# Sliding-window extraction: VectorE's plain row copies go from identity shuffles to copies, and one of them takes ScalarE's quarter

## The chip, the cores and the metric

The kernel runs on one core of a Trainium2 chip. The metric is the device time of one execution in microseconds; three runs of the kernel before took 187.24, 187.06 and 187.02 us, a median of 187.06 us.

Three engines matter here: VectorE (DVE), ScalarE (ACT) and GpSimd (POOL). TensorE does nothing. POOL issues most of the DMAs, SyncE (SP) and ACT the rest. Sixteen DMA engines move the bytes between device memory and the on-chip memory (SBUF), which has 128 partitions.

## The reference

The input `x` has 16 images of 64 channels of 64 x 64 float32. Every 8 x 8 window with stride 4 is copied out, 15 x 15 windows per image, each with all channels:

```
n_h = (h - window_size) // stride + 1
n_w = (w - window_size) // stride + 1
result = np.zeros((batch, n_h, n_w, c, window_size, window_size), dtype=np.float32)
for i in range(n_h):
    for j in range(n_w):
        h_start = i * stride
        w_start = j * stride
        result[:, i, j] = x[:, :, h_start:h_start + 8, w_start:w_start + 8].copy()
```

Nothing is calculated; it is a movement of data. The input is 16.78 MB and the output 58.98 MB, as neighbouring windows overlap: 3600 windows (16 x 225) of 64 x 8 x 8 float32, 16384 bytes each. One window is one row of the output when that is seen as a matrix, and is contiguous there.

## The kernel before

**The input on chip.** The tile `L` holds all of `x`. Each image is cut into 4 bands of 16 image rows (`HQ = 4`) and 2 halves of 32 channels (`CH = 2`). Partition `ch*64 + b*4 + q` holds channel half `ch` of image `b`, band `q`: 32 channels x 16 rows x 64 columns. The loads are issued by POOL, SP and ACT at the start (`load`, L58, and L112); the first channels of each partition come by way of two of the output buffers and are copied into `L` at L126.

**The output buffers.** There are four, `G0` to `G3`, used in turn by `tile_()`. A buffer has 128 partitions of one whole window each (64 channels x 8 x 8, 16384 bytes). So one buffer takes 128 windows, and one store, an indirect DMA issued by POOL (L138, `scatter`), writes each partition to the output row that an index list gives (`idx_y`, `idx`, `idx_lo`, `idx_hi`). A row whose index lies beyond the output is dropped. A buffer is filled again only when its store has landed, which the framework enforces with semaphores.

**The tiles in their order.** With `s` the number of a window's first row within the band in units of 4 (0 to 3) and `j` the window's column:

- *Parts* (`part`, L197), six of them: the windows of half of the images for two columns and `s` = 0 and 1. Each is 8 copies of 32 partitions, 3 by ACT and 5 by DVE. The first three are made as soon as half of the input is there, the other three each go before one of three plain units.
- *Plain units* (`unit` with `s == 0`), eight of them: partitions 0 to 63 take the windows with `s` = 0 and partitions 64 to 127 those with `s` = 1, for one column. For either half there are two copies, one from each channel half of `L`, because a window needs both. The first copy of each half is ACT's, the second is `copies[0]` or `copies[1]`. The first three plain units use DVE copies for these, the next four the default of `unit`, and the last one divides both between ACT and DVE.
- *Cross units* (`unit` with `s == 2`), fifteen of them, in groups of three with a plain unit after each group: one half of the partitions takes `s` = 2, the other `s` = 3. The `s` = 2 half is made by ACT (two copies of 64 x 2048, L158). Windows with `s` = 3 reach into the next band: their upper four rows come from the same partition and their lower four from the next one. So for each channel half there is a plain copy of four rows (L160) and then a shuffle over partitions (L161) with the mask `nxt`, which takes each partition's rows from its neighbour. Band 3 has no next band, so 16 of the 128 rows of such a tile are dropped by the index list (`idx_hi`, `idx_lo`); the halves change places from one cross unit to the next.
- *Last column*: two tiles of 64 partitions, filled at L245 by ACT and DVE in 16 copies and stored by SP (L247), no longer by POOL.

**What sets the order.** Each engine works in the order of the program. There is no planner; the four buffers and the semaphores on them are all that couples the engines. POOL does nothing after the loads but wait for a tile's fill and issue its store.

**The plain copies of VectorE.** `shf` does a plain copy with a shuffle whose mask is the identity (L168). `mix` is a function made by `split`: ACT copies the first quarter of the channels (8 of 32, L172) and `shf` the other 24. Cross units before call `fill(..., (shf, mix))` for their `s` = 3 half: the four plain rows of the first channel half are all DVE's, those of the second are divided by `mix`. Plain units by default have `shf` in one half and `mix` in the other.

Of the kernel before, what the change touches and what calls it, by code (L numbers as in the profile page):

```python
# [10 lines left out]
def kernel(  # L11
# [21 lines left out]
    CL = C // CH  # L33
# [4 lines left out]
    HP = P // CH  # L38
# [70 lines left out]
    for ch in range(CH):  # L109
        for q in range(HQ):  # L110
            s = S[ch][QP + q : QP + q + (B - 1) * HQ + 1 : HQ]
# [25 lines left out]
    def scatter(g, ix, j, s):  # L137
        st = nc.gpsimd.indirect_dma_start(  # L138
            out=o_v,
            out_offset=bass.IndirectOffsetOnAxis(ap=ix[:, 0:1], axis=0),  # L140
            in_=g.rearrange("p c r w -> p (c r w)"),
            in_offset=None,
            element_offset=(s * NW + j) * CFREE,
            bounds_check=B * NWIN - 1,
            oob_is_err=False,
        )
        free(st)

    def fill(g, half, s, j, lo, n, copies):

        d = slice(half * HP + lo, half * HP + lo + n)
        cols = slice(j * ST, j * ST + WS)
        for ch in (half, 1 - half):
            f = slice(ch * HP + lo, ch * HP + lo + n)
            cs = slice(ch * CL, (ch + 1) * CL)
            copy = copies[ch != half]
            if s < NSLOT - 1:
                copy(out=g[d, cs, :, :], in_=L[f, :, s * ST : s * ST + WS, cols])  # L158
            else:
                copy(out=g[d, cs, 0:ST, :], in_=L[f, :, s * ST : RB, cols])  # L160
                nc.vector.stream_shuffle(out=g[d, cs, ST:WS, :], in_=L[f, :, 0:ST, cols], mask=nxt)  # L161

    act, dve = nc.scalar.copy, nc.vector.tensor_copy
# [6 lines left out]
    def split(k, other):  # L170
        def both(out, in_):
            act(out=out[:, 0:k], in_=in_[:, 0:k])  # L172
            other(out=out[:, k:], in_=in_[:, k:])  # L173

        return both

    mix = split(CL // 4, shf)


    EARLY = 3  # L180
    ACT_C = 12
    at = 0
# [1 line left out]
    def tile_():  # L184
        nonlocal at
        at += 1
        return G[(at - 1) % NG]

    def part(y, j):
        g = tile_()  # L190
        order = [(d, ch) for ch in range(CH) for d in range(P // QP)]
        for n, (d, ch) in enumerate(order):
            s, dj = d // NY, d % NY
            cols = slice((j + dj) * ST, (j + dj) * ST + WS)
            f = (ch * NY + y) * QP
            tc.keep_in_program_order(
                (act if n % 3 == 0 else dve)(  # L197
                    out=g[d * QP : (d + 1) * QP, ch * CL : (ch + 1) * CL, :, :],
                    in_=L[f : f + QP, :, s * ST : s * ST + WS, cols],
                )  # L200
            )
        scatter(g, (idx_y0, idx_y1)[y], j, 0)

    crossed = 0

    def unit(j, s, copies=(shf, mix)):
        nonlocal crossed
        g = tile_()
        if s == 0:
            fill(g, 0, 0, j, 0, HP, (act, copies[0]))  # L210
            fill(g, 1, 1, j, 0, HP, (act, copies[1]))
            scatter(g, idx, j, s)
        else:

            turn = 1 - crossed % 2
            crossed += 1
            fill(g, turn, s, j, 0, HP, (act, act))
            fill(g, 1 - turn, s + 1, j, 0, HP, (shf, mix))
            scatter(g, (idx_hi, idx_lo)[turn], j, s)

    for n in range(EARLY):
# [1 line left out]
    plain = [(j, 0) for j in range(2 * EARLY, NW - 1)]  # L223
    cross = [(j, 2) for j in range(NW)]
    for n in range(EARLY):
        part(1, 2 * n)
        unit(*plain.pop(0), (dve, dve))
    while plain:
        for w in cross[:3]:
            unit(*w)  # L230
        cross = cross[3:]
        unit(*plain.pop(0), *([] if len(plain) else [(split(ACT_C, shf), split(ACT_C, dve))]))
# [3 lines left out]
    j = NW - 1  # L236
    for s in range(2):
        g = tile_()
# [44 lines left out]
```

## Time and profile before

| | |
|---|---|
| Median of three runs | 187.06 us (187.02 to 187.24) |
| Profiled execution, its own time | 187.55 us |
| Its span on the core | 185.8 us |
| DVE busy, instructions | 146.8 us, 205 |
| ACT busy, instructions | 146.7 us, 96 |
| POOL busy, instructions | 48.6 us, 50 |
| Moved by DMA | 75.81 MB, 408 GB/s over the span |

The span is the time between the first and the last thing that the profiler saw on the core; 1.75 us of the execution's time lie around it. Busy times are of one execution. A group of instructions is written as line, engine, operation, output <- input, the shapes (partitions x elements), the number of them, then busy microseconds and the mean of one in nanoseconds, then the idle time just before them. In a table by stretches each row has the bounds in us from the start of the span, the busy time and the number of instructions of DVE, ACT and POOL, a clock (of TensorE, here without meaning), the share of the 16 DMA engines that was busy, and the rate at which bytes moved. "To landing" is the time from the issue of a DMA to the arrival of its last byte.

### The profile page before, as it was taken

To read this page: it belongs to the slowest core of one execution; us is meant where nothing else is said; L and a number is where in the kernel's file an instruction comes from. 1 tells how busy PE (TensorE), PEld (TensorE's weight loads), DVE (VectorE), ACT (ScalarE), POOL (GpSimd) and SP (SyncE) were. 2 spreads that over 40 slices of the span, in tenths; PEclk is the share of its full clock that TensorE was granted. 3 is DMA by queue.
4 is the path that set the end of the run, shared out by engine and by line. 5 is a ranking of instruction groups with operands and counts; after the bars stand their busy time and mean duration, and the time that the engine had idled before them with its cause. 6 is when DMAs were issued, how large, how long until landed. Compare 5 with 4: busy or idle time off the path is not lost.

```text
span 185.8 us, 578 instructions
## 1 busy us (share of the span) xinstructions
DVE 146.8 (79%) x205; ACT 146.7 (79%) x96; POOL 48.6 (26%) x50
## 2 busy tenths in 40 slices
DVE  5045007999998979799999999999999999999600
ACT  0069207999699999987999999998999999899600
POOL 7505222313417170522121112111211121112000
DMA  4999999999999999999999999999999999999994
GB/s 156 331 409 402 399 397 401 382 388 424 427 427 437 429 430 430 434 434 430 422 439 423 430 430 430 437 427 430 434 430 418 437 423 430 423 423 423 413 441 187
DMA packets 11300, 75.81 MB, mean 408 GB/s; under 512 B 3600, under 2 KB 3600, under 8 KB 7696
## 3 DMA queue, kind: packets, MB, share of 16 engines
q0 software_dynamic: 9296, 66.86, 86.2%
q1 hardware_dynamic: 1680, 7.86, 10.6%
q10 hardware_dynamic: 320, 1.05, 1.8%
q14 instruction: 4, 0.03, 0.0%
HBM read 16.78 MB, written 62.91 MB: 429 GB/s over the span
## 4 chain that ended last, share of the span: by engine, by line
DMA 42%; DVE 36%; issue 9%; ACT 5%; ACTq 1%; SPq 0%; POOLq 0%; DVEq 0%
DVE G L168 17%; DMA out_dram<-G,idx_y 15%; DMA out_dram<-G,idx 13%; DMA L<-in_x_dram 11%; DVE G L161 10%; DVE G L197 9%; DMA G<-in_x_dram 4%; ACT G L245 3%; ACT G L158 1%; ACT G L172 1%; ACTq L278 0%; DVE G L158 0%; SPq L58 0%; ACTq L112 0%; POOLq L138 0%
## 5 line engine op out<-in xcount | busy, mean ns | idle before, releaser
L158 ACT COPY G<-L 64x2048 f32<-64x2048 f32 x46 | 87.2, 1896 | 5.0 <-DMA out_dram<-G,idx 2.5
L168 DVE STREAM_SHUFFLE G<-L 64x1024 f32<-64x1024 f32 (+4 forms) x39 | 53.0, 1358 | 1.2
L197 DVE COPY G<-L 32x2048 f32<-32x2048 f32 x30 | 36.6, 1220 | 15.3 <-DMA L<-in_x_dram 12.8
L197 ACT COPY G<-L 32x2048 f32<-32x2048 f32 x18 | 34.1, 1897 | 11.5 <-DMA L<-in_x_dram 11.0
L161 DVE STREAM_SHUFFLE G<-L 64x1024 f32<-64x1024 f32 x30 | 38.4, 1281 | 0.0
L138 POOL DMA_INDIRECT out_dram<-G,idx_y x6 | 11.3, 1887 | 25.1 <-DVE G L197 25.1
L58 POOL DMA_DIRECT2D L<-in_x_dram x16 | 11.9, 755 | 20.0 <-DMA L<-in_x_dram 19.5
L138 POOL DMA_INDIRECT out_dram<-G,idx_lo x8 | 7.7, 961 | 31.0 <-DVE G L161 23.3
L138 POOL DMA_INDIRECT out_dram<-G,idx x8 | 10.6, 1331 | 17.9 <-DVE G L168 6.8
L138 POOL DMA_INDIRECT out_dram<-G,idx_hi x7 | 6.7, 961 | 26.6 <-DVE G L161 22.8
L126 DVE COPY L<-G 32x4096 f32<-32x4096 f32 x2 | 4.6, 2286 | 8.3 <-DMA G<-in_x_dram 8.3
L172 ACT COPY G<-L 64x256 f32<-64x256 f32 (+2 forms) x21 | 10.2, 484 | 0.5
L126 ACT ACT_TABLE_LOAD x1 | 1.3, 1283 | 11.1 <-DMA G<-in_x_dram 11.1
L158 DVE COPY G<-L 64x2048 f32<-64x2048 f32 x6 | 7.3, 1222 | 0.2
L126 ACT COPY L<-G 32x4096 f32<-32x4096 f32 x2 | 7.2, 3603 | 0.0
L245 ACT COPY G<-L 32x768 f32<-32x768 f32 x8 | 6.6, 830 | 0.1
L245 DVE COPY G<-L 32x1280 f32<-32x1280 f32 x8 | 6.5, 818 | 0.1
L168 DVE LOAD_MASK_SELECT G<-L x39 | 0.2, 6 | 1.4 <-DMA out_dram<-G,idx_y 1.2
L72 DVE TENSOR_SCALAR tb<-pi 128x1 int32<-128x1 int32 x1 | 0.2, 154 | 1.0 <-POOL pi L69 1.0
L173 DVE COPY G<-L 64x1280 f32<-64x1280 f32 x1 | 0.9, 877 | 0.0
L78 DVE TENSOR_TENSOR th<-tc,tq 128x1 int32<-128x1 int32 x2 | 0.3, 156 | 0.0
L75 DVE TENSOR_SCALAR th<-tc 128x1 int32<-128x1 int32 x2 | 0.3, 154 | 0.0
(21 smaller groups left out, 3.0 us busy)
## 6 DMA issues: line engine op xcount, KB each, us to landing
L<-in_x_dram POOLq DMA_DIRECT2D x10, 896.0 KB, 19.9
L<-in_x_dram SPq DMA_DIRECT2D x6, 768.0 KB
out_dram<-G SPq DMA_DIRECT2D x2, 1024.0 KB, 10.1
G<-in_x_dram ACTq DMA_DIRECT2D x4, 256.0 KB, 8.3
G<-in_x_dram SPq DMA_DIRECT2D x4, 256.0 KB, 8.8
L<-in_x_dram POOLq DMA_DIRECT2D x6, 128.0 KB, 18.8
out_dram<-G,idx POOLq DMA_INDIRECT x8, 13.0
out_dram<-G,idx_lo POOLq DMA_INDIRECT x8, 10.0
```

Source lines behind the costliest of these rows:

```text
L58: eng.dma_start(out=L[p0 : p0 + QP - HQ + 1 : HQ, c0:c1, :, :], in_=x_v[ch, y, q, :, c0:c1, :])
L75: nc.vector.tensor_scalar(out=d[:, :], in0=a[:, :], scalar1=float(m), scalar2=None, op0=ALU.mult)
L78: nc.vector.tensor_tensor(out=d[:, :], in0=a[:, :], in1=b[:, :], op=op)
L126: (nc.scalar.copy, nc.vector.tensor_copy)[ch](out=L[d, 0:FC, :, :], in_=S[ch][f])
L138: st = nc.gpsimd.indirect_dma_start(out=o_v, out_offset=bass.IndirectOffsetOnAxis(ap=ix[:, 0:1], axis=0), in_=g.rearrange("p c r w -> p (c ...
L158: copy(out=g[d, cs, :, :], in_=L[f, :, s * ST : s * ST + WS, cols])
L161: nc.vector.stream_shuffle(out=g[d, cs, ST:WS, :], in_=L[f, :, 0:ST, cols], mask=nxt)
L168: nc.vector.stream_shuffle(out=out, in_=in_, mask=same)
L172: act(out=out[:, 0:k], in_=in_[:, 0:k])
L173: other(out=out[:, k:], in_=in_[:, k:])
L197: (act if n % 3 == 0 else dve)(out=g[d * QP : (d + 1) * QP, ch * CL : (ch + 1) * CL, :, :], in_=L[f : f + QP, :, s * ST : s * ST + WS, cols],)
L245: copy(out=g[d, ch * CL + c0 : ch * CL + c1, :, :], in_=L[f, c0:c1, s * ST : s * ST + WS, cols])
```

## The change

`mix` is gone. Wherever a default plain unit or a cross unit used `shf` or `mix`, it now uses `dve`, VectorE's `tensor_copy`. So the four plain rows of the `s` = 3 half are two DVE copies of 64 x 1024 (L160), where there had been a shuffle of 64 x 1024, a shuffle of 64 x 768 and an ACT copy of 64 x 256; and a default plain unit has two DVE copies of 64 x 2048, where there had been shuffles of 64 x 2048 and 64 x 1536 and an ACT copy of 64 x 512. The shuffles with `nxt` (L161) stay, and so does the last plain unit with its one `shf`. Nothing else moves: the tiles, their order, the stores and the loads are the same.

```diff
-    mix = split(CL // 4, shf)
-
-
     EARLY = 3
     ACT_C = 12
     at = 0
...
-    def unit(j, s, copies=(shf, mix)):
+    def unit(j, s, copies=(dve, dve)):
         nonlocal crossed
         g = tile_()
         if s == 0:
...
             turn = 1 - crossed % 2
             crossed += 1
             fill(g, turn, s, j, 0, HP, (act, act))
-            fill(g, 1 - turn, s + 1, j, 0, HP, (shf, mix))
+            fill(g, 1 - turn, s + 1, j, 0, HP, (dve, dve))
             scatter(g, (idx_hi, idx_lo)[turn], j, s)
...
     for n in range(EARLY):
         part(1, 2 * n)
-        unit(*plain.pop(0), (dve, dve))
+        unit(*plain.pop(0))
```

## The prediction

> **What bounds the kernel now.** I read the page's slices first: do the engines or the DMAs fill the span?
>
> ```profile
> span 185.8 us, 578 instructions
> DVE  5045007999998979799999999999999999999600
> ACT  0069207999699999987999999998999999899600
> DMA  4999999999999999999999999999999999999994
> ```
>
> All three rows are full from about 32 us on, so busy shares do not decide. The DMA row is full from 5 us to the end. So I asked for a table by stretches, whose last two columns are the DMA engines' busy share and the rate.
>
> ```profile
> 36.00:57.00 21.00, 19.93 (x17) 19.09 (x11) 7.60 (x4) 1.00 1.03 413
> 57.00:80.00 23.00, 20.07 (x20) 22.49 (x13) 9.48 (x5) 1.00 1.01 432
> 80.00:100.00 20.00, 19.35 (x31) 17.92 (x14) 3.85 (x4) 1.00 1.01 432
> 100.00:120.00 20.00, 19.66 (x31) 19.51 (x15) 3.88 (x5) 1.00 1.00 429
> 120.00:140.00 20.00, 19.74 (x31) 19.06 (x15) 4.76 (x5) 1.00 1.01 431
> 140.00:160.00 20.00, 19.68 (x33) 19.11 (x14) 3.85 (x4) 1.00 1.01 428
> 160.00:172.00 12.00, 11.81 (x17) 11.10 (x11) 2.96 (x3) 1.00 1.00 419
> ```
>
> The share is 1.00 or more everywhere and the rate is 432 GB/s both where DVE does copies only (57 to 77 us) and where it shuffles (80 to 100). The DMA engines are never without work, and their bytes set the end.
>
> How much work lies ahead of them? That is the time from a store's issue to its landing, asked for by windows (first 57 to 78 us, then 100 to 125, then 150 to 172):
>
> ```profile
> out_dram<-G,idx POOLq DMA_INDIRECT x3, 14.3
> ...
> out_dram<-G,idx_hi POOLq DMA_INDIRECT x3, 11.0
> out_dram<-G,idx_lo POOLq DMA_INDIRECT x2, 10.6
> ...
> out_dram<-G,idx_lo POOLq DMA_INDIRECT x2, 8.9
> out_dram<-G,idx_hi POOLq DMA_INDIRECT x1, 9.5
> ```
>
> A cross store moves 112 rows of 16384 bytes, 1.835 MB, 4.27 us at 430 GB/s; a plain one 2.097 MB, 4.88 us. So 14.3 us is three stores in the queue, 9 us two. The queue shrinks, because filling is slower than storing. In the timeline the plain stores at 96.68 and 115.22 us are one group (three cross tiles, one plain) apart: 18.54 us, while its bytes take 3 x 4.27 + 4.88 = 17.7 us. That is 0.85 us lost per group, 4.2 us over the five groups, about the 5 us by which landing got shorter. The kernel ends before the queue is used up. A faster fill thus buys a longer queue first, and no time.
>
> The groups that the change touches, and the nearest ones for prices:
>
> ```profile
> L161 DVE STREAM_SHUFFLE G<-L 64x1024 f32<-64x1024 f32 x30 | 38.4, 1281 | 0.0
> L168 DVE STREAM_SHUFFLE G<-L 64x1024 f32<-64x1024 f32 x15 | 19.3, 1285 | 0.5
> L168 DVE STREAM_SHUFFLE G<-L 64x768 f32<-64x768 f32 x15 | 15.0, 998 | 0.5
> L138 POOL DMA_INDIRECT out_dram<-G,idx_y x6 | 11.3, 1887 | 25.1 <-DVE G L197 25.1
> L138 POOL DMA_INDIRECT out_dram<-G,idx_lo x8 | 7.7, 961 | 31.0 <-DVE G L161 23.3 <-ACT G L172 3.9 <-ACT G L158 3.8
> L158 DVE COPY G<-L 64x2048 f32<-64x2048 f32 x6 | 7.3, 1222 | 0.2
> L245 DVE COPY G<-L 32x1280 f32<-32x1280 f32 x8 | 6.5, 818 | 0.1
> ```
>
> **The change part by part.** Everything before the first cross tile at 77 us stays as it is.
>
> DVE in cross units, 15 of them. Removed: 15 x (1.285 + 0.998) = 34.2 us. Added: 30 copies of 64 x 1024. The trace has none; from 818 ns at 1280 elements and 1222 ns at 2048, 0.526 ns an element, it is 818 - 256 x 0.526 = 683 ns. Upper bound: 1285 ns, if pieces of four rows do not reach a copy's rate. I take 683, since both copy rows read pieces of eight elements out of 64 just as this one will: 20.5 us (at most 38.6).
>
> DVE in the four default plain units. The shuffles of 64 x 2048 (2429 ns) and 64 x 1536 (1860 ns) go, 17.2 us; two copies of 1222 ns come, 9.8 us.
>
> DVE in all: 51.4 us out, 30.3 us in, 21.1 us less busy (at the upper bound 3.0 us).
>
> ACT loses the L172 copies of 64 x 256 (15 x 402 ns) and of 64 x 512 (4 x 617 ns): 8.5 us.
>
> Fill per tile. A cross tile takes DVE 4.72 us now (shuffles starting at 100.68 and 105.40) and then 2 x (0.683 + 1.281) = 3.93 us; ACT 4.26 us now (100.26 to 104.52), then 3.83 us. A group then takes 3 x 3.93 + 3.83 = 15.6 us, in place of 18.54, against 17.7 us of bytes. At the upper bound DVE takes 3 x 5.1 + 2.4 = 17.7 us: still no slower than before.
>
> What is late next is a buffer. Filling 2.1 us a group faster than storing, it soon runs into the rule that a buffer's last store must have landed; from then on DVE and ACT wait, some 8 to 10 us each over five groups, and three stores are always in the queue. All of the 21 and 8.5 us goes into these waits. Worth on the path: 0.
>
> The end. The last tile's buffer comes free with the store of the tile four before it; behind that lie a cross store, a plain one and 2 x 1.05 MB, 4.27 + 4.88 + 4.88 = 14.0 us. Its fill is 4 x 0.83 us of ACT work at L245, so SP issues with more than 8 us of work still queued. Nothing there moves the end.
>
> POOL's issues. The 20 stores from 82 us on are the ones touched. An issue beside shuffles took 961 ns, beside DVE copies 1887 ns (1758 to 2443 by the groups' extremes). Bounds for each: 0 and +1.48 us; I take +0.5 us, for copies are now about a third of DVE's work there, not nearly all of it. Only POOL waits for this: nothing is behind an issue but the next, 4.4 us later. Hidden by the queue: at the shortest landing, 8.5 us, some 4 us of other stores were ahead; with three stores it will be about 8 us. If that cover were gone, 20 x 0.5 = 10 us.
>
> The Trainium skill has a rule against this change (SBUF — State Buffer, "Who interferes with whom"): a VectorE copy in a two-port mode holds the port pair that GpSimd needs to write descriptors, and GpSimd is blocked until it ends. The longer issues beside copies agree with it. By the rule alone the sum would have the issue delays on top; the 432 GB/s of 57 to 80 us, where copies and long issues stood side by side, says that they are covered.
>
> The rate. It sagged from 432 to 429, 431, 428 and 419 GB/s as the queue got shorter. If a long queue restores 432, the gain is at most (3 x 20 + 1 x 20 + 4 x 20 + 13 x 12) / 432 = 0.73 us. The other bound is 0: the sag may belong to the addresses. The end is set by the one DMA engine that finishes last; chaining the trace's packets end to start, it has some 0.3 us of packets slower than 0.61 us after 140 us. I take half of that, 0.15 us.
>
> Sum: 187.55 - 0.15 = 187.40 us against the profiled execution, which is 0.49 us above the median; against the median 187.06 - 0.15 = 186.9 us.
>
> **The rivals.**
> *Faster: the sag goes away in full.* For it: the rate fell as landing fell from 14.3 to 9 us. Against: the last engine has only some 0.3 us to win. Time: 187.06 - 0.73 = 186.33 at best, 186.75 with 0.3 us.
>
> *Slower: VectorE's copies hold up the issues, and the DMAs run dry.* Place: L138, from 82 us on. For it: 961 against 1887 ns. Against: 432 GB/s beside those 1887 ns. It decides once an issue is late by more than the work queued in front of it, 4 us by the shortest landing; measured delays reach 1.5 us. If uncovered in full at the measured difference, 20 x 0.926 = 18.5 us, 205.6 us; a single uncovered delay of 0.93 us gives 188.0 us. This is the time that the port rule gives in the Trainium skill's page named above, if no queue hides it. A milder form, a few DMA engines dry for a moment at some issues, costs 0.4 to 1 us.
>
> *The change does not do what it says: four-row copies stay at 1285 ns.* Then fill equals bytes, 17.7 us a group, and the queue merely stops shrinking: 187.06 us, no change again.
>
> **How the numbers follow.** A measurement of this kernel tells about 0.2%, 0.37 us, from no change. The forecast, bytes bind and the end stays within that (186.7 to 187.4), has 0.55 and slow four-row copies 0.07, which gives the same time: 0.62. The sag gone by more than 0.37 us: 0.20. Issues uncovered: 0.18, mostly in the mild form. The range 186.5 to 187.8 leaves out the lower half of the faster case and the worse half of the slower one. The likeliest case's own range is 186.7 to 187.4.
>
> **What would show it.** After the change: DMA share 1.00 and 428 to 432 GB/s in every stretch from 57 to 172 us; DVE about 126 us busy, ACT about 138; L160 DVE copies at about 683 ns; cross stores landing after 12 to 14 us, not 9 to 11; ACT and DVE waiting for landed stores by some 10 us each (ACT 4.0 us and DVE 3.0 us now); issues of cross stores between 1.0 and 1.9 us. Wrong, if the DMA share falls below 0.98 in a stretch after 80 us, if issues take over 4 us, or if the rate with a full queue is not that of before.

## The result and the profile after

The changed kernel takes 187.61 us (median of 8 runs, 187.34 to 187.74), the kernel before, run beside it on the same chip, 187.02 us (8 runs, 186.71 to 187.24). The ratio is 1.0027, with a 95% interval of 1.0014 to 1.0039. That is slower, by about a quarter of a per cent: inside the range, but on the other side of the 0.2% that I had set for "no change", where I had forecast 0.15 us less. The execution that was profiled took 187.59 us, with the same span as the one before.

The slices of the page, answering to the first lines shown of before:

```profile
span 185.8 us, 506 instructions
DVE  5044008999998969877768957985897497666600
ACT  0069109996999989977798978988897797689700
DMA  5999999999999999999999999999999999999993
```

DVE and ACT now have holes all along from about 60 us on; the DMA row is full as before. The table by stretches (DVE, ACT and POOL busy with instruction counts, then clock, DMA share, GB/s):

```profile
57.00:80.00 23.00, 20.10 (x20) 21.80 (x12) 7.89 (x5) 1.00 1.01 431
80.00:100.00 20.00, 14.63 (x22) 15.97 (x10) 5.66 (x5) 1.00 1.01 432
100.00:120.00 20.00, 16.54 (x26) 17.81 (x10) 4.91 (x5) 1.00 1.01 431
120.00:140.00 20.00, 15.86 (x24) 17.06 (x10) 6.04 (x5) 1.00 1.00 427
140.00:160.00 20.00, 15.40 (x24) 16.70 (x10) 4.91 (x5) 1.00 1.01 425
160.00:172.00 12.00, 6.96 (x9) 9.37 (x9) 2.03 (x2) 1.00 1.00 421
172.00:186.00 14.00, 2.94 (x4) 3.59 (x5) 0.00 (x0) 1.00 0.78 334
```

DVE does some 16 us of work in 20 where it did 19.7, and the DMA engines are busy all the same, at 1.00 or more. The rate does not go up with the longer queue: 427 and 425 GB/s from 120 to 160 us, where the kernel before had 431 and 428 (in a second trace of each, told of below, 431 and 423 against 429 and 427). That is the first place where the forecast's small term is seen to fail. The groups:

```profile
L160 DVE COPY G<-L 64x1024 f32<-64x1024 f32 x30 | 21.1, 703 | 14.1 <-DMA out_dram<-G,idx_hi 7.6
L138 POOL DMA_INDIRECT out_dram<-G,idx_lo x8 | 9.0, 1128 | 29.8 <-DVE G L161 23.0
L138 POOL DMA_INDIRECT out_dram<-G,idx_hi x7 | 8.7, 1246 | 21.5 <-DVE G L161 21.5
L158 ACT COPY G<-L 64x2048 f32<-64x2048 f32 x46 | 87.2, 1896 | 15.3 <-DMA out_dram<-G,idx 7.6
```

The new copies take 703 ns (683 was taken), and both engines now stop for landed stores. Issue to landing, first 57 to 78 us, then 100 to 125, then 150 to 172:

```profile
out_dram<-G,idx POOLq DMA_INDIRECT x3, 14.8
...
out_dram<-G,idx_hi POOLq DMA_INDIRECT x3, 13.3
out_dram<-G,idx_lo POOLq DMA_INDIRECT x2, 12.5
...
out_dram<-G,idx_lo POOLq DMA_INDIRECT x2, 13.7
out_dram<-G,idx_hi POOLq DMA_INDIRECT x1, 14.8
```

Three stores lie in the queue to the end, where two did. And from the view of waits:

```profile
ACT G L158 <- DMA out_dram<-G,idx: 7.6, 6, 2.5
DVE G L160 <- DMA out_dram<-G,idx_hi: 7.6, 6, 2.3
DVE G L168 <- DMA out_dram<-G,idx: 2.5, 1, 2.5
```

(columns: sum, number, longest). Over all stores ACT waits 14.9 us in place of 4.0, DVE 24.7 in place of 3.0: DVE is 19.9 us less busy and waits 21.7 us more, so what it saved went straight into waiting. Its last line is one wait of 2.5 us, at 163 us; that one is not explained by bytes, and it is where the search began.

**Where the time is.** A transfer is spread over 16 DMA engines, and the trace has the landing of each one's share. I took two clocks from it: the mean of the 16, and the last of the 16, both from the landing of the first plain unit's store (at about 71 us) to the end. "Lag" is the distance from the mean of the 16 to the last at the last store.

```
                 mean: from-to  takes   last: from-to  takes   lag   execution
before           70.78-183.93  113.15   72.02-184.89  112.87  0.96   187.55
before_again     70.63-183.82  113.19   71.70-184.57  112.87  0.75   187.22
after            70.30-183.58  113.27   71.46-184.94  113.48  1.36   187.59
after_again      70.23-183.44  113.21   71.54-184.94  113.40  1.50   187.60
copies_quarter   70.16-183.46  113.30   71.28-184.81  113.53  1.35   187.47
shuffles_half    70.51-183.78  113.27   71.41-184.71  113.29  0.93   187.36
copies_padded    70.41-183.66  113.25   71.27-184.51  113.24  0.85   187.16
before_fill22    70.57-183.83  113.27   71.88-184.94  113.05  1.11   187.59
before_fill108   70.40-183.75  113.35   71.30-184.59  113.29  0.84   187.25
after_fill22     70.41-183.69  113.28   71.55-185.23  113.68  1.54   187.88
after_fill64     70.61-183.80  113.19   72.08-185.33  113.25  1.53   187.99
after_fill108    70.37-183.82  113.45   72.25-186.68  114.42  2.86   189.34
after_lo9        70.65-183.79  113.14   72.52-184.89  112.37  1.10   187.55
```

The mean engine takes 113.2 us whatever the fill does: 113.15 and 113.19 before, 113.27 and 113.21 after. In the changed kernel it is even done earlier, 183.58 us in place of 183.82 (before_again), as it began 0.33 us earlier. What is later is the last engine: 184.94 in place of 184.57, 0.37 us, and the executions differ by exactly that, 187.59 - 187.22. So the loss is the distance from the mean engine to the last, 1.36 and 1.50 us in the changed kernel against 0.96 and 0.75 before. The page's share and rate don't show it: they are averages over the sixteen.

Nor is an engine without work for a moment, which an average could hide. Counted packet by packet, all sixteen engines have one under way from 57 to 178 us in the changed kernel; what is missing adds up to 0.01 us of one engine's time (0.05 in after_again). In the kernel before it is 1.0 and 0.6 us, all of it behind 140 us, where its queue is shortest.

The landings of the very last store, engine by engine, sorted, in us after the first of them:

```
before_again  0.0 0.1 0.1 0.1 0.2 0.2 0.2 0.2 0.2 0.2 0.4 0.7 0.7 0.8 1.1 1.1
after         0.0 0.0 0.1 0.3 0.3 0.3 0.8 0.8 0.9 1.1 1.1 1.1 1.1 1.2 1.6 2.2
after_again   0.0 0.1 0.2 0.2 0.3 0.3 0.5 0.5 1.0 1.1 1.1 1.1 1.4 1.4 1.8 2.4
```

One engine ends 0.6 us behind the next in both traces of the changed kernel; in before_again the last two end together.

### The profile page after: what moved, and what is told of

Read it like the earlier page. It is cut to its first block, busy times and chain, and to the rows that moved or that the text cites. A ratio compares the mean times of both kernels' runs of the same rounds, so it can differ in the third digit from the quotient of the medians.

```text
span 185.8 us, 506 instructions
## 1 busy us (share of the span) xinstructions
DVE 126.9 (68%) x167; ACT 138.1 (74%) x77; POOL 51.5 (28%) x50
## 4 chain that ended last, share of the span: by engine, by line
DMA 72%; DVE 11%; ACT 5%; issue 3%; POOL 2%; ACTq 1%; DVEq 0%; PEldq 0%
DMA out_dram<-G,idx 23%; DMA out_dram<-G,idx_hi 21%; DMA L<-in_x_dram 13%; DVE G L194 10%; DMA out_dram<-G,idx_lo 7%; DMA out_dram<-G,idx_y 6%; ACT G L242 3%; POOL L L58 2%; ACT G L158 1%; ACT G L172 1%; ACTq L275 1%; DVE G L158 0%; DVEq L194 0%; DVE G L160 0%; POOL pi L69 0%
## 5 line engine op out<-in xcount | busy, mean ns | idle before, releaser
L161 DVE STREAM_SHUFFLE G<-L 64x1024 f32<-64x1024 f32 x30 | 38.2, 1273 | 0.0
L160 DVE COPY G<-L 64x1024 f32<-64x1024 f32 x30 | 21.1, 703 | 14.1 <-DMA out_dram<-G,idx_hi 7.6
L158 DVE COPY G<-L 64x2048 f32<-64x2048 f32 x14 | 17.1, 1222 | 4.5 <-DMA out_dram<-G,idx 4.2
L138 POOL DMA_INDIRECT out_dram<-G,idx_lo x8 | 9.0, 1128 | 29.8 <-DVE G L161 23.0
L138 POOL DMA_INDIRECT out_dram<-G,idx x8 | 10.4, 1301 | 19.9 <-ACT G L158 13.4
L138 POOL DMA_INDIRECT out_dram<-G,idx_hi x7 | 8.7, 1246 | 21.5 <-DVE G L161 21.5
L172 ACT COPY G<-L 64x768 f32<-64x768 f32 x2 | 1.7, 830 | 0.0
L168 DVE STREAM_SHUFFLE G<-L 64x1280 f32<-64x1280 f32 x1 | 1.6, 1606 | 0.0
```

Source lines behind the costliest of these rows:

```text
L138: st = nc.gpsimd.indirect_dma_start(out=o_v, out_offset=bass.IndirectOffsetOnAxis(ap=ix[:, 0:1], axis=0), in_=g.rearrange("p c r w -> p (c ...
L168: nc.vector.stream_shuffle(out=out, in_=in_, mask=same)
```

## The experiments

Unless another kernel is named, ratios are to the kernel before, run beside it on the same chip, with the 95% interval behind. The expectations name rival theories of the loss by letters. A: one last DMA engine sets the time (A1: it is held back by a late fetch of VectorE's instructions, of which more below; what A2 is, each text says). B: VectorE's copies beside POOL's issues. C: the longer queue of stores. BC: copies and queue cost a little each, fetches nothing.

**Both kernels again.** No edit; how much does a copy of the same kernel differ?

> The kernel before, unchanged, for a second trace of it: the first was of an execution of 187.55 us, above all the times listed for that kernel. Both theories expect 187.0 us and a ratio of 1.000 +- 0.001. If the last of the sixteen DMA engines sets the time (theory A), the last store's sixteen landings, one for each DMA engine, are closer together here than in the changed kernel, by about 0.5 us between the median engine and the last.

> The changed kernel once more, for a second trace. All theories expect 187.5 to 187.6 us, ratio 1.0027 +- 0.001. Theory A (one DMA engine is held back): in its trace one engine lands 0.6 us or more behind the next in the last store, as in the first trace. Theories B (copies beside POOL's issues) and C (three stores in the queue): all engines land later together, and the rate between 100 and 172 us is 425 to 430 GB/s against 430 in the other kernel.

Measured: before_again 187.15 us (12 runs, 186.72 to 187.82), 1.0010 [0.9997, 1.0024]. after_again 187.71 us (9 runs, 187.52 to 187.83), 1.0038 [1.0026, 1.0051]. The loss repeats, and the kernel against itself comes out 0.1% apart, which its interval does not tell from nothing. The changed kernel's times are also the tighter: 17 runs within 0.49 us, while before_again alone spreads over 1.1. In the timeline of after_again the wait at 163 us is there again (start, duration, engine, line, instruction, then the wait ahead of it):

```profile
161.69 0.97 POOL L138 DMA_INDIRECT out_dram<-G,idx_lo  x1 [3.77 <-DVE G L161]
163.39 1.90 ACT L158 COPY G<-L 64x2048 f32<-64x2048 f32 x1 [2.48 <-DMA out_dram<-G,idx]
```

POOL's issue is over within 1 us and POOL had waited 3.77 us for the fill before it. ACT waits for a store that was issued long ago, one of whose sixteen shares is late.

**The copies without the queue.** The changed kernel's copies stay; useless work in front of the fills is to make them about as slow as in the kernel before. What it writes is written over by the fill.

```diff
         if s == 0:
+            if len(plain) < 5 and plain:
+                act(out=g[0:HP, 0:8], in_=L[0:HP, 0:8, 0:WS, j * ST : j * ST + WS])
             fill(g, 0, 0, j, 0, HP, (act, copies[0]))
...
+            cols = slice(j * ST, j * ST + WS)
+            a, v = (slice(h * HP, (h + 1) * HP) for h in (turn, 1 - turn))
+            act(out=g[a, 0:4], in_=L[0:HP, 0:4, s * ST : s * ST + WS, cols])
+            shf(out=g[v, 0:16, 0:ST], in_=L[0:HP, 0:16, (s + 1) * ST : RB, cols])
             fill(g, turn, s, j, 0, HP, (act, act))
```

> The changed kernel with its copies, but with extra work that makes the fill as slow as before: in each cross tile a shuffle of 64 x 512 on VectorE and a copy of 64 x 256 on ScalarE into the places that the real fill then overwrites, in four plain tiles a ScalarE copy of 64 x 512. DVE per cross tile 3.9 + 0.75 = 4.7 us, so stores land after 9 to 11 us at the end again. Theory B (the copies): still slow, 187.5 us, ratio 1.0027. Theory C (the long queue): back to 187.0 us, ratio 1.000. Theory A (one DMA engine, by where instruction fetches and other small things fall): anywhere from 186.9 to 187.6, with the last engine's lag showing which.

**The queue without the copies.** Shuffles of half the channels, which take about as long as copies of all; the other half of these plain rows is left out.

```diff
+    def half(out, in_):
+        shf(out=out[:, 0 : CL // 2], in_=in_[:, 0 : CL // 2])
+
-    def unit(j, s, copies=(dve, dve)):
+    def unit(j, s, copies=(half, half)):
...
-            fill(g, 1 - turn, s + 1, j, 0, HP, (dve, dve))
+            fill(g, 1 - turn, s + 1, j, 0, HP, (half, half))
...
-        unit(*plain.pop(0))
+        unit(*plain.pop(0), (dve, dve))
```

> The kernel before with its identity shuffles, but of 16 of the 32 channels only, and without ScalarE's quarter; the other channels of those rows are left out, so part of the output is not written with the right windows. VectorE takes about 2 x (0.75 + 1.28) = 4.05 us for a cross tile, so the queue is as long as in the changed kernel (landing 12 to 14 us), with no copies beside the cross stores. Theory B: 187.0 us, ratio 1.000. Theory C: 187.5 us, ratio 1.0027. Theory A: either, by the last engine's lag.

Measured: copies_padded 187.24 us, 1.0018 [1.0005, 1.0031]; shuffles_half 187.31 us, 1.0021 [1.0008, 1.0034]. shuffles_half is what it was meant to be, copies_padded only in part: its queue stays longer than was expected (9 to 11 us). Stretches 140 to 160 us of copies_padded, then of shuffles_half:

```profile
140.00:160.00 20.00, 17.10 (x30) 18.34 (x14) 5.71 (x5) 1.00 1.01 425
```

```profile
140.00:160.00 20.00, 15.67 (x31) 16.75 (x10) 4.65 (x5) 1.00 1.01 426
```

and issue to landing from 150 to 172 us of copies_padded, shuffles_half and before_again:

```profile
out_dram<-G,idx_lo POOLq DMA_INDIRECT x2, 11.6
```

```profile
out_dram<-G,idx_lo POOLq DMA_INDIRECT x2, 12.7
```

```profile
out_dram<-G,idx_lo POOLq DMA_INDIRECT x2, 8.8
```

DVE is busy in shuffles_half as in the changed kernel, and its queue is as long; in copies_padded it is in between. Either comes out above the kernel before and below the changed one, and by 0.08 and 0.11% above before_again, which no interval here tells from nothing. Their last engines lag by 0.85 and 0.93 us, as before. The two runs don't separate copies and queue cleanly: they also move VectorE's instruction fetch (see below) to 143 and 140 us, where the kernel before has it.

**The quarter back to ScalarE; shuffles without ScalarE's quarter.** In copies_quarter only shuffles have become copies, in shuffles_all only ACT's quarter has moved.

```diff
+    mix = split(CL // 4, dve)
-    def unit(j, s, copies=(dve, dve)):
+    def unit(j, s, copies=(dve, mix)):
...
-            fill(g, 1 - turn, s + 1, j, 0, HP, (dve, dve))
+            fill(g, 1 - turn, s + 1, j, 0, HP, (dve, mix))
```

(in shuffles_all `(shf, shf)` in the same two places; both give `(dve, dve)` to the first three plain units, as before)

> One part of the change alone: copies in place of the identity shuffles, ScalarE keeps its quarter (copies of 64 x 1024 and 64 x 768, 64 x 2048 and 64 x 1536 on VectorE). VectorE takes 0.69 + 1.28 + 0.56 + 1.28 = 3.8 us for a cross tile, ScalarE 4.25 us, a group 3 x 4.25 + 4.4 = 17.2 us against 17.7 us of bytes: the queue stays about as it is after the first stage. VectorE has as many instructions as in the changed kernel. Theory A1: fetch at about 160 us, 187.5 to 187.7 us. Theory B (copies): 187.6. Theory C (long queue, buffer waits): 187.3 to 187.6.

> The other part alone: VectorE takes over ScalarE's quarter, but by shuffles (64 x 1024 twice, 64 x 2048 twice). VectorE then takes 4 x 1.25 = 5.0 us for a cross tile and 4.85 for a plain one, a group 19.9 us against 17.7 us of bytes, so the queue of 14 us shrinks by 11 us over five groups and is some 4 us at the end. All theories: 187.0 us if the queue just lasts, up to 189 if it does not; by A1 with the fetch at 140 us the last engine is not held back.

Measured: copies_quarter 187.71 us, 1.0039 [1.0022, 1.0056], as slow as the whole change, so the loss does not need the move of ACT's quarter. It has as many VectorE instructions as the changed kernel, and the same late fetch at 162 us (see below). shuffles_all 191.56 us, 1.0238 [1.0213, 1.0264], more than was expected. Its stretches:

```profile
100.00:120.00 20.00, 19.70 (x29) 17.91 (x10) 3.85 (x4) 1.00 1.00 429
120.00:140.00 20.00, 19.74 (x29) 16.25 (x10) 3.85 (x4) 1.00 0.95 400
140.00:160.00 20.00, 19.70 (x29) 15.63 (x9) 3.85 (x4) 1.00 0.90 380
```

Issue to landing, 125 to 150 us:

```profile
out_dram<-G,idx_hi POOLq DMA_INDIRECT x2, 7.3
```

Here the fill takes 19.9 us a group against 17.7 us of bytes, and the queue does run out: after 120 us, when landing has come down to some 7 us, DMA engines begin to stand idle. I had expected the queue of 14 us to last longer; engines run dry not when issue to landing has come down to nothing but at about 7 us, of which 4.3 to 4.9 us are the store's own bytes (an estimate, from the prediction's sizes and 430 GB/s). This bounds the cover that the prediction counted on: 8.8 us in the kernel before is near the edge, 12 to 15 us in the changed one is far from it.

**Which engines get the rows that are dropped.** A cross tile has 16 rows that its index list drops, and so 112 that are written. With the halves in the other order, each of eight DMA engines gets two rows of 16384 bytes more over the whole kernel, and each of the other eight two fewer.

```diff
-            turn = 1 - crossed % 2
+            turn = crossed % 2
```

(in after_lo9 `turn = 1 - crossed % 2 if crossed < 14 and crossed != 7 else 1`, which moves rows the other way)

> The same exchange in the kernel before. Theory A: there too the last engine takes 6 rows of an idx_lo store, so 0.8 to 1.2 us slower, 187.8 to 188.2 us, ratio 1.004 to 1.006. Theories B and C: 187.0 us, ratio 1.000.

> The changed kernel with the two halves of the cross tiles exchanged: the first cross unit uses idx_hi, so idx_hi drops its 16 rows eight times and idx_lo seven (now seven and eight). The work in all is the same, but eight of the sixteen DMA engines get two rows of 16384 bytes more (1.22 us) and the other eight two fewer. In the traces the engine that lands last takes 6 rows of an idx_lo store (its landings are then 3.65 us apart, not 4.85), so it is one of those that get more. Theory A (the one last engine sets the time): about 1.2 us slower than the changed kernel, 188.9 us, ratio 1.010. Theories B (copies) and C (long queue), by which the DMAs are late together: no change, 187.6 to 187.8.

> The changed kernel with idx_lo used nine times and idx_hi six: the engines with the last one get two rows fewer, the other eight two rows more. Theory A: the last engine ends 1.2 us earlier, but the other eight, now some 1.4 to 2.2 us ahead of it, end 1.2 us later; 0 to 0.3 us faster than the changed kernel, 187.3 to 187.6 us. Theories B and C: 187.6 to 187.8.

Measured: before_flip 188.65 us, 1.0084 [1.0064, 1.0104]; after_flip 189.53 us, 1.0137 [1.0112, 1.0161], 1.8 us over after_again; after_lo9 188.44 us, 1.0083 [1.0065, 1.0101]. In the flipped kernel's last store the engines have parted in two groups of eight (us after the first landing; the second group only):

```
after_flip    3.4 3.5 3.5 3.8 3.9 4.0 4.5 4.6   (the first eight: 0.0 to 0.8)
```

The same bytes, the same instructions, nearly the same mean engine (it takes 113.19 us in after_flip, 113.52 in before_flip), and 1.6 and 1.8 us more. A packet of 16384 bytes takes 0.611 us on an engine, so two of them are 1.22 us; the rest of the loss is not explained. So the last engine sets the time, not the sum of bytes over the rate. after_lo9 was to relieve the last engine and be 0 to 0.3 us faster; it came out 0.8 us slower than the changed kernel. That the other eight became last instead is likely but not shown: its one trace is of its fastest execution (187.55 us, the others 188.28 or more), where nine engines land within 0.5 us of the last.

**The place of VectorE's instruction fetches.** The trace also has the packets that bring instructions: 8192 bytes each, 309 ns, on one of the same 16 DMA engines. VectorE fetches about every 128 of its instructions. (Every trace has two more such packets in this part, at about 90 and 96 us in nearly all; they stay there whatever VectorE runs, so I take them for those of POOL and ACT: they fall at the 66th or 67th instruction of POOL and the 66th to 73rd of ACT, as VectorE's first does at its 65th or 66th.) The packets around a fetch of VectorE are slowed: the next takes 0.95 to 0.99 us in place of 0.611, and in most kernels with the longer queue one that starts 1.5 us ahead takes 0.88 to 0.99. In the kernel before VectorE's fetches lie at about 62 and 140 us; in the changed one, which gives VectorE fewer instructions in the same time, at 60 and 162. The wait of 2.5 us at 163 us is the second: the last share of that store landed 6.31 us after the last of the store before (6.29 in after_again), where 4.8 to 5.0 is usual for a full tile, and the last engine's distance to the second rose from 0.04 to 1.32 us (0.03 to 1.31). In the kernel before, the step across its fetch at 140 us is 5.26 and 5.15 us, and the distance goes from 0.02 to 0.29 and from 0.39 to 0.32: the engine that was hit was not far in the last place. So my theory became: the loss is this fetch, so late that the engine can't recover. Useless instructions of VectorE at the start, where it waits for the first loads, move all later fetches and nothing else:

```diff
+    spare = ipool.tile([P, 22], i32, name="spare")
+    for k in range(22):
+        nc.vector.tensor_scalar(out=spare[:, k : k + 1], in0=pi[:, :], scalar1=1, scalar2=1, op0=ALU.logical_shift_right, op1=ALU.bitwise_and)
```

(64 or 108 in place of 22 in the others; one starts every 60 ns or so, and all of them lie before 9 us)

> The changed kernel with 22 tiny VectorE instructions (128 x 1) put into its idle time before the first data has come, into a tile that nobody reads. They cost nothing there (about 3.3 us of an idle stretch) but move every later instruction of VectorE 22 places on, so that the instruction fetch of 8192 bytes that falls at 162 us in the changed kernel falls at about 140 us, where it is in the kernel before. Theory A1 (the late fetch holds back the DMA engine that ends last): 187.2 to 187.3 us, ratio 1.001 to 1.002. Theories A2 (the order of the last tiles, whose fill now waits for buffers) and C (the long queue): unchanged, 187.6 to 187.7 us, ratio 1.003 to 1.004.

> The same with 64 tiny instructions: the fetch of 162 us moves to about 100 us, that of 61 us into the loads. Theory A1: 187.0 to 187.3 us. Theories A2 and C: 187.6 to 187.7 us.

> The kernel before with the 22 tiny VectorE instructions in its idle start. Its two instruction fetches move from 62 and 141 us to about 36 and 125 us; fill, queue and copies stay as they are. Theory A2 (where the fetches fall decides which DMA engine is last): the time may move by up to 0.6 us either way, 186.8 to 187.6. Theory BC (copies and long queue each cost a little, fetches nothing): 187.0 us, ratio 1.000.

> The kernel before with 108 tiny instructions (16 us of an idle start of 26 us): one more fetch in the loads, then fetches at about 63 and 162 us, as in the changed kernel. Theory A2: as slow as the changed kernel, 187.5 to 187.7 us, ratio 1.003. Theory BC: 187.0 us, ratio 1.000.

> The changed kernel with 108 tiny instructions: one more fetch in the loads, then one at about 61 us and none after it, as the program ends before the next would be due. Theory A2: without the late fetch the last engine ends 0.6 us or more earlier, 187.0 to 187.2 us. Theory BC: 187.6 to 187.7 us.

Measured (VectorE's fetches as seen in each trace):

```
                 fetches at (us)    median us   ratio to before
after            60, 162            187.61      1.0027 [1.0014, 1.0039]
after_fill22     35, 144            187.80      1.0043 [1.0029, 1.0057]
after_fill64     8, 113             187.80      1.0040 [1.0026, 1.0055]
after_fill108    9, 82, 181         188.54      1.0073 [1.0047, 1.0098]
before           62, 140            -           -
before_fill22    35, 127            187.58      1.0032 [1.0014, 1.0050]
before_fill108   8, 80, 152         187.36      1.0015 [1.0001, 1.0030]
```

The theory as it stood falls: with the fetch at 144 or 113 us the changed kernel is not faster. But the traces speak less against the fetch than the times do. In after_fill22 the fetch at 144 us met the last engine again: the step there is 6.30 us, and the distance to the second goes from 0.49 to 1.91 us. The same stands in copies_quarter (a step of 6.24 us, 0.07 to 1.25). In these two and the two traces of the changed kernel 0.53 to 0.75 us of that distance is left at the end, about what was lost. after_fill64 is the one against it: its fetch at 113 us put the lag up by only some 0.3 us, no later step up to 176 us is above 5.01 us, and its last engine lags by 1.53 us all the same.

A fetch can cost what was lost. after_fill108 was expected to have none after 61 us; it has one at 181, on an engine that was already 1.71 us behind the second to last. That distance rose to 3.91, and the kernel lost 0.9 us more. And the kernel before, with 22 instructions that do nothing, lost 0.32%, as much as the whole change lost. 108 of them cost it 0.15%, less than was expected, though that is more useless work; the two intervals overlap.

**16 instructions fewer on VectorE.** This was another try at moving the late fetch: 16 of the 20 small operations that compute the index lists go from VectorE to POOL, behind its loads. There they stand beside VectorE's copies and before the first stores, and the run showed something else than was asked: the price of the ports with no queue ahead.

```diff
-        nc.vector.tensor_scalar(out=d[:, :], in0=a[:, :], scalar1=float(m), scalar2=None, op0=ALU.mult)
+        nc.gpsimd.tensor_scalar(out=d[:, :], in0=a[:, :], scalar1=float(m), scalar2=None, op0=ALU.mult)
...
-        nc.vector.tensor_tensor(out=d[:, :], in0=a[:, :], in1=b[:, :], op=op)
+        nc.gpsimd.tensor_tensor(out=d[:, :], in0=a[:, :], in1=b[:, :], op=op)
```

> The changed kernel with 16 of the 20 small index instructions moved from VectorE to POOL, behind its loads. VectorE's program is 16 instructions shorter, so its last instruction fetch (8192 bytes at 162 us, after which one DMA engine is 1.3 us behind the others) comes later or not at all. Theory A: if it does not come, 187.0 us or less, ratio 0.998 to 1.000; if it still comes, 187.6. Theories B and C: 187.6 to 187.8 us whatever the fetch does.

Measured: 194.19 us, 1.0389 [1.0363, 1.0416], far outside what any theory had said, so it tells nothing of the fetch (which still came, at 182 us). The prediction's slower rival needs VectorE's copies to hold up POOL where no queue covers it, and here is such a place. The timeline of POOL, four of its lines:

```profile
35.59 1.17 POOL L99 TENSOR_SCALAR idx_y<-t 128x1 int32<-128x1 int32 x1
...
42.95 0.19 POOL L102 TENSOR_TENSOR th<-tc,tq 128x1 int32<-128x1 int32 x1
43.22 1.07 POOL L112 TENSOR_SCALAR idx_y<-idx_y 128x1 int32<-128x1 int32 x1
...
46.91 2.38 POOL L140 DMA_INDIRECT out_dram<-G,idx_y  x1 [0.19 <-DVE G L196]
```

An operation on one element a partition takes 1.02 to 1.30 us while VectorE copies. Two took 0.19 and 0.20 us: one at 58.87 us, when VectorE was idle, and the one at 42.95 us, which began in the gap between two copies (one ended at 42.94, the next started at 42.97). The Trainium skill (SBUF — State Buffer, "Who interferes with whom") says that GpSimd is blocked until VectorE's copy in a two-port mode ends; this agrees. The first store is issued at 46.91 us where it was 35.46, and the stretch shows what that does to the DMA engines:

```profile
36.00:57.00 21.00, 19.27 (x17) 16.90 (x10) 19.46 (x16) 1.00 0.85 331
```

So the rival's mechanism is real, its price is about 1 us an operation, and it is paid on the path as soon as no queue lies ahead. In the changed kernel the issues of cross stores took 1128 and 1246 ns on average, 0.17 and 0.29 us more than before, and each of these stores landed 12.4 us or more after its issue, so that two others were ahead of it.

## Why the prediction was wrong, and where it was right

*What bounds the kernel.* Right, and stronger than said: the mean DMA engine takes 113.1 to 113.5 us in all thirteen traces of the table and in both flipped kernels, and 118.1 in shuffles_all, whose queue ran dry.

*The costs of VectorE and ScalarE.* Right: L160 at 703 ns (683 taken; the bound of 1285 was not touched), DVE 126.9 us busy (126), ACT 138.1 (138).

*What is late next.* Right in kind: the fill runs into its buffers, three stores stay queued, cross stores land after 12.4 to 14.8 us, 13.3 in the middle (12 to 14). Right in size for ACT, which waits 10.9 us more; wrong for DVE, which waits 21.7 us more, where I had said some 8 to 10. The prediction contradicts itself there, as its next sentence puts all of DVE's 21 us into waits. I had given both engines the time by which a group's fill became shorter, and forgotten that DVE then has no work in the rest either: what an engine saves off the path it waits, all of it.

*The end, SP's issues.* Right: SP issues at 172.3 and 175.7 us, 0.7 us later than before, with stores queued ahead.

*POOL's issues.* Right in sign, under the value taken: +0.17 and +0.29 us (0.5), hidden. The rival with uncovered issues did not come about, in its mild form neither, though its 0.4 to 1 us is about what was lost: the DMA share is never below 1.00 from 57 to 172 us, and packet by packet no engine was without work for more than 0.01 us in all.

*The rate.* This is the step that failed, the term of -0.15 us. I took the sag from 432 to 419 GB/s for a thing of the short queue, between 0 and 0.73 us to win. A queue of 12 to 15 us left it in place: 425 and 423 GB/s from 140 to 160 us in the two traces of the changed kernel, 428 and 427 in those of the kernel before; only from 160 to 172 us was there a little more, 421 and 424 against 419 twice. So the short queue is not what makes most of the sag. The longer one even brought slow packets of its own: from 120 to 172 us the ten traces of kernels whose cross stores land after 11 us or more there have 37 to 57 packets of 16384 bytes that take 0.675 to 0.8 us in place of 0.611, while the kernel before, its three variants and shuffles_all have 2 to 10. shuffles_half, without full-speed copies beside its cross stores, has 52 of them, and copies_quarter, where ACT keeps its quarter, 51, so they go with the queue; why they come only behind 120 us is open. And I wrote that the end is set by the DMA engine that finishes last, and then bounded that engine only from one side, by its own slow packets after 140 us, as if it could only win. The bound on the other side was in the same trace: a difference between engines of the order of 1 us at the last landing, against which 0.15 us is nothing. Measured, the last engine was 0.37 us later although the mean one was 0.24 us earlier. The forecast of no change thus held for the transfers as a whole and failed for the one engine on which the kernel ends. That the time lies inside the stated range all the same is luck: the room above 187.4 us was kept for late issues, which cost nothing.

What stays open is why one engine lags by 1.35 to 1.54 us in the profiled executions with full-speed copies and a full queue (after, after_again, copies_quarter, after_fill22, after_fill64; 2.86 in after_fill108, and 1.10 in the fastest execution of after_lo9), and by 0.75 to 1.11 in the kernel before, with and without useless instructions, and in the two that have only one of copies and queue. Two things are seen to put an engine back: a fetch that meets the engine already last, in four of these traces, and the slow packets of the longer queue. Which of them made the loss in the changed kernel is not shown. The fetch has the better case, but after_fill64 lags without such a step, and copies_padded and shuffles_half, which are nearly as fast as the kernel before, changed the fetch together with the copies or the queue.

No version here beats the kernel before.

## What to carry to other kernels

In a kernel bound by stores, time saved on the engines that fill goes into waits for buffers, and the last few tenths of a per cent are set by how evenly the bytes, the slow packets and the instruction fetches lie on the DMA engines: look at the landing of each engine's share, not at the mean share and rate, and bound it from both sides before forecasting "no change" within 0.2%. A queue of stores hides longer issues as long as it is well above one store's own transfer (here: hardly a gap while stores landed 8.5 us or more after their issue, gaps at about 7). An edit that changes only the number of instructions moves the instruction fetches, so a difference of 0.3% needs a control that moves them too before it is put down to the edit.

## What the runs showed of the hardware

- Instruction fetches take time on the DMA engines that move the data. One is 8192 bytes, about every 128 instructions of VectorE; with its neighbours' slowing (0.309 us, and 0.951 and 0.885 in place of 0.611) it puts that engine back by 0.6 to 1 us, an estimate from these sums. The last engine's distance to the second rose by 1.2 to 1.4 us at such a store, by 2.2 in after_fill108. 22 instructions in idle time cost the kernel before 0.32% [0.14, 0.50].
- With three stores queued, 37 to 57 packets of 16384 bytes took 0.675 to 0.8 us in place of 0.611 between 120 and 172 us; with two, 4 to 10.
- Two rows of 16384 bytes more on each of eight DMA engines, and two fewer on each of the other eight, cost 1.6 and 1.8 us in a kernel of 187.
- GpSimd's operations on 128x1 take 0.19 to 0.20 us when no copy of VectorE is under way and 1.02 to 1.30 us beside one; the issue of an indirect store takes 1.1 to 1.25 us on average where copies are a third of VectorE's work, 0.96 beside shuffles.
